# A hybrid decoder trunk: the convolution's inputs projected ahead of the index queries

## The chip, the cores and the metric

One core of a Trainium2 chip runs the whole program as one launch. The metric is the device time of that launch in microseconds, as the median of the runs shown. TensorE is called PE here, VectorE DVE, ScalarE ACT, GpSimd POOL and SyncE SP.

## The reference

Two layers work on 512 tokens of 1024 features, in float32. One projection of the normalized input gives every column that three token mixers need; their outputs are gated, summed and projected back, and a convolutional feed-forward block follows.

```python
z = h @ w_in + b_in
u_pool, u_conv, q, k, v, qi, ki, wi, gates = split_cols(z, IN_SIZES)
y_pool = pool_mixer(u_pool, pool_w, pool_scale) @ w_pool_out
y_conv = conformer_conv(u_conv, ...) @ ...       # GLU, 31 causal taps per channel, LayerNorm, silu
y_attn = dsa_attention(q, k, v, qi, ki, wi) @ w_attn_out
merged = g[:, :, 0] * y_pool + g[:, :, 1] * y_conv + g[:, :, 2] * y_attn
h = layer_norm(ALPHA * h + merged @ w_o);  h = layer_norm(ALPHA * h + conv_ffn(h))
```

In the attention an indexer scores all visible keys of a query with eight small heads, `sum_h w_h * relu(qi_h . ki)`; the best 128 keys are kept and only these take part in the softmax.

## The kernel before, in words

All activations lie with features on the partitions and the 512 tokens along the free axis. A product in float32 precision is made of three matmuls: each operand is split into a rounded high part and the rest, and hi x hi, hi x lo and lo x hi are added in PSUM (`proj`, L283 to L292). A weight chunk of 128 x 1024 gives one output tile of 128 columns: 8 steps of 3 matmuls, 24 in all. Weights come in the order of use from one tensor (`Weights`, L55): SP loads a chunk, ACT rounds it to `w_hi` (L74), DVE, or POOL for a few chunks, forms `w_lo` (L78). Four split chunks fit in SBUF, and a chunk is asked for two chunks ahead.

`mix` (L356) is the stage that the change touches. It projects, in this order: the index keys, the keys and the first half of the pooling channels (a head that starts while the norm before is still running); the four index query tiles, with 384 columns since the first 128 queries need no index; the second half of the pooling channels; two gate tiles and two value tiles of the convolution; the attention's values; then gate tiles and attention queries. A query or key tile is rotated (`rotate`, L411): ACT copies it, SP issues four transfers that swap half-heads, POOL multiplies by the sine (L408), DVE adds (L418), and ACT and DVE split the sum (`stack`, L423).

Beside these tiles run pieces of work that are written as generators and pumped by `step(ca, cb)`: `ca` is an amount for the index and attention work (`index_gen` L468, `attn_gen` L674), `cb` a number of pieces of the convolution (`conv_gen` L581). One piece of the convolution is one tap of one channel half. Of 31 taps the first is an ACT operation, every fourth is an accumulation on DVE in PSUM (L599, L602), and the others, 23 a half and 46 a layer, are a product on ACT (L596, two buffers `cvt`) and an addition on POOL (L597).

`pool_gen` (L510) makes the windowed sums of the pooling branch: per channel half a few additions on POOL (L517 to L527), a scaled subtraction on DVE (L529), a split (L534), three matmuls each into a bank `pb_p`, and a scaled split of the result into two `gbt` pairs, `pool_out` (L550, L551). `y_small` (L724) multiplies the output weights with `pool_out`; this happens first at L733, right behind the first gate tile (L732).

PSUM is handed out by tag: `pb_a` three banks, `pb_s` two (index and attention scores), `pb_p` two, `pb_v` one. `pb_p` serves every second query tile, the DVE taps' accumulator, `pool_gen`'s products, the transposed values and attention's transposes.

The framework takes the instructions in the order in which they are written as priorities, and sets the final order on each engine by a timeline of its own. On the chip each engine works through its list in that order.

Of the kernel before, what the change touches and what calls it, by code (L numbers as in the profile page):

```python
# [8 lines left out]
F32 = mybir.dt.float32  # L9
# [6 lines left out]
P = 128  # L16
# [73 lines left out]
def trunk_kernel(ctx, tc, x, positions, w, poolw, params, lnv, cons, out):  # L90
# [208 lines left out]
    def in_tile(c0=0, tag="a"):  # L299
        wt = W.take()  # L300
        o = bank(tag)
        in_part(o, wt, c0, c0, L)
        return o
# [52 lines left out]
    def mix(l, head, prev, ln, nxt):  # L356
        es = ExitStack()
        with es:
# [5 lines left out]
            def q_slot(tag, dt=F32R):  # L364
                return slot(tag, {"qa": 6, "qb": 4, "qc": 4}[tag], dt)

            def t_slot(dt=F32):
                return slot("t", 4, dt)
# [10 lines left out]
            def pb(ct):  # L379
                return par[:, l, PO_B + ct:PO_B + ct + 1]  # L380

            def hb(ct):
                return half_par[:, l, ct:ct + 1]
# [39 lines left out]
            def stack(a, s0, s1):  # L423
                for s, r, q in ((s0, UP, DN), (s1, DN, UP)):
                    A.activation(s[r], a[r], AF.Copy)
                    split_lo(s[q], a[r], s[r])
                return s0, s1
# [30 lines left out]
            up = [p_slot()]  # L458
            G.memset(up[0][:, 0:16], 0.0)
            A.activation(up[0][:, 16:], head.os[2], AF.Identity, bias=pb(6))  # L460
            for j in range(4):
                o = in_tile(P, "a" if j % 2 == 0 else "p")
                tag = "qa" if j < 2 else "qb"
                qi.append(stack(rotate(o, pb(2 + j), P, p_slot), q_slot(tag)[:, 0:L - P], q_slot(tag)[:, 0:L - P]))

            masks = [tri] + [None] * 3

# [89 lines left out]
                pass  # L557


            hp = []  # L560
            ths = []
            for c in range(2):
                o = in_tile()
                th = t_slot()
                A.activation(th, o, AF.Tanh, bias=hb(8 + c), scale=0.5)
                ths.append(th)
                step(3.0, 0)
            for c in range(2):
                o = in_tile()
                aa = t_slot()  # L570
                A.activation(aa, o, AF.Identity, bias=hb(10 + c), scale=0.5)
                hc = c_slot()[:, 0:CW - 1 + L]
                G.memset(hc[:, 0:CW - 1], 0.0)
                V.scalar_tensor_tensor(out=hc[:, CW - 1:], in0=ths[c], scalar=1.0, in1=aa,
                                       op0=ALU.add, op1=ALU.mult)
                hp.append(hc)
                step(2.5, 0)

            conv_out = []

            def conv_gen():  # L581
                accs = []
                for c in range(2):
                    acc, pacc = bank("p"), c_slot()[:, 0:L]

                    def tap(i):
                        k = PO_CW + c * CW + i
                        return par[:, l, k:k + 1]

                    A.activation(pacc, hp[c][:, 0:L], AF.Identity, scale=tap(0),  # L590
                                 bias=par[:, l, PO_CB + c:PO_CB + c + 1])
                    started = False
                    for i in range(1, CW):
                        if i % 4 != 0:
                            tm = slot("cvt", 2)
                            A.activation(tm, hp[c][:, i:i + L], AF.Copy, scale=tap(i))  # L596
                            G.tensor_tensor(out=pacc, in0=pacc, in1=tm, op=ALU.add)  # L597
                        elif not started:
                            V.tensor_scalar(acc, hp[c][:, i:i + L], tap(i), None, op0=ALU.mult)  # L599
                            started = True  # L600
                        else:
                            V.scalar_tensor_tensor(out=acc, in0=hp[c][:, i:i + L], scalar=tap(i),  # L602
                                                   in1=acc, op0=ALU.mult, op1=ALU.add)
                        yield 1
                    V.tensor_tensor(out=pacc, in0=acc, in1=pacc, op=ALU.add)
                    accs.append(pacc)
                    yield 1
                xn = []
                for bp in range(2):
                    pt = bank("p")  # L610
                    for bb in range(2):
                        b = bp * 2 + bb
                        for c in range(2):
                            T.transpose(pt[:, (bb * 2 + c) * P:(bb * 2 + c + 1) * P],
                                        accs[c][:, b * P:(b + 1) * P], ident)
                    xt = u_slot()
                    for bb in range(2):
                        seg = pt[:, bb * 256:(bb + 1) * 256]
                        st = sm.tile([P, 6], F32, name="c_st")
                        V.bn_stats(st, seg)  # L620
                        mv = sm.tile([P, 2], F32, name="ln_mv")
                        V.bn_aggr(mv, st)
                        ve = sm.tile([P, 1], F32, name="ln_ve")
                        V.tensor_scalar(ve, mv[:, 1:2], EPS, None, op0=ALU.add)
                        rs = sm.tile([P, 1], F32, name="ln_rs")
                        G.tensor_tensor(out=rs, in0=ve, in1=mhalf, op=ALU.pow)
                        V.tensor_scalar(xt[:, bb * 256:(bb + 1) * 256], seg, mv[:, 0:1], rs,
                                        op0=ALU.subtract, op1=ALU.mult)
                    xn.append(xt)
                    yield 1  # L630
                for c in range(2):
                    pt = bank("p")
                    for b in range(NB):
                        T.transpose(pt[:, b * P:(b + 1) * P],
                                    xn[b // 2][:, (b % 2) * 256 + c * P:(b % 2) * 256 + (c + 1) * P], ident)
                    hg = half_par[:, l, 41 + c:42 + c]
                    hbb = half_par[:, l, 43 + c:44 + c]
                    th = u_slot()
                    A.activation(th, pt, AF.Tanh, bias=hbb, scale=hg)
                    y2 = u_slot()  # L640
                    A.activation(y2, pt, AF.Identity, bias=hbb, scale=hg)
                    V.scalar_tensor_tensor(out=y2, in0=th, scalar=1.0, in1=y2, op0=ALU.add, op1=ALU.mult)
                    hi, lo = c_slot(F32R)[:, 0:L], c_slot(F32R)[:, 0:L]
                    A.activation(hi, y2, AF.Copy)
                    split_lo(lo, y2, hi)
                    conv_out.append((hi, lo))
                    yield 1

            bgb.append(conv_gen())


            o = in_tile()
            t = t_slot()
            A.activation(t, o, AF.Identity, bias=pb(12))
# [4 lines left out]
            vpv = vps.rearrange("p (b g d) -> p g b d", b=NB, g=2)  # L659
            A.activation(v_st[:, :, :, 0:64], vpv, AF.Copy)  # L660
            split_lo(v_st[:, :, :, 64:128], vpv, v_st[:, :, :, 0:64])
            step(1.5, 0)
            qa_hi = slot("qa_hi", 1, F32R, [P, 4, L])
            qa_lo = slot("qa_lo", 1, F32R, [P, 4, L])
            qa = (qa_hi, qa_lo)
# [170 lines left out]
def _chunks(a, np):  # L836
# [19 lines left out]
    for l in range(DEPTH):  # L856
# [6 lines left out]
            small.append(a[name][l].reshape(2, P, 2, 4, P).transpose(2, 1, 3, 0, 4).reshape(2, P, D))  # L863
        wa = a["w_attn_out"][l].reshape(2, 4, 64, D).transpose(1, 0, 2, 3).reshape(4, P, 4, 2, P)
        wa = wa.transpose(2, 1, 3, 0, 4).reshape(4, P, D)
        seq = [tiles[i] for i in (0, 1, 6, 2, 3, 4, 5) + tuple(range(7, 13))]
        for br in range(2):
            for hh in range(2):
                seq.append(small[br][hh])
# [66 lines left out]
```

## Time and profile before

| | us |
|---|---|
| median of 3 runs (1494.2 to 1494.74) | 1494.37 |
| the profiled execution, its own time | 1493.34 |
| its span | 1491.5 |
| PE busy | 1448.0 (97%) |
| DVE busy | 956.7 (64%) |
| ACT busy | 678.6 (45%) |
| POOL busy | 525.2 (35%) |
| DMA, mean over the span | 97 GB/s |

The span is the time from the first to the last instruction; the profiled execution's own time is 1.8 us longer. PE is counted busy as long as a matmul is in flight, and matmuls overlap, so its share says little: the number of matmuls started in a stretch says more. The mean granted clock of PE is 0.997 of full speed. The first layer's mixing stage lies at about 40 to 375 us, the second's at 770 to 1105 us.

### The profile page before, as it was taken

How to read it: one execution, taken by the hardware profiler on the slowest of the kernel's cores; microseconds unless marked ns; L12 is line 12 of the kernel's file. 1: busy time of each engine (PE TensorE's matmuls, PEld its weight loads, DVE VectorE, ACT ScalarE, POOL GpSimd, SP SyncE). 2: the span in 40 equal slices, each digit the busy share in tenths (PEclk: the TensorE clock that was granted, in tenths of full speed). 3: DMA queues.
4: the chain of work that ended last, by engine and by line, in shares of the span. 5: the costliest groups of instructions: out<-in, count | busy, mean ns of one | idle time of the engine just before them, and what ended most of it. 6: DMA issues, size and time to landing. Idle time of an engine off the chain costs nothing.

```text
span 1491.5 us, 18622 instructions
## 1 busy us (share of the span) xinstructions
PE 1448.0 (97%) x6850; PEld 1209.1 (81%) x6850; DVE 956.7 (64%) x1600; ACT 678.6 (45%) x1064; POOL 525.2 (35%) x395
## 2 busy tenths in 40 slices
PE   5999999999999999999999989999999999999997
PEld 5887878878888888888898878888788888888885
DVE  6789998746666555523267999966566655554234
ACT  5677555532544444421256774554334444443110
POOL 2459624129471111100133894220667311111004
PEclk9999999999999999999999999999999999999999
DMA  4432332223233323333224233222324333333331
GB/s 153 135 103 85 92 107 71 71 85 99 91 115 107 93 93 97 99 99 100 85 90 139 72 96 110 72 71 85 99 71 149 109 108 93 95 98 99 100 99 57
DMA packets 45019, 145.02 MB, mean 97 GB/s; under 512 B 6144, under 2 KB 7808, under 8 KB 44928
## 3 DMA queue, kind: packets, MB, share of 16 engines
q1 hardware_dynamic: 41472, 138.27, 30.3%
q10 hardware_dynamic: 3456, 5.57, 1.1%
q8 instruction: 54, 0.88, 0.2%
q14 instruction: 37, 0.30, 0.1%
HBM read 137.00 MB, written 2.10 MB: 93 GB/s over the span
## 4 chain that ended last, share of the span: by engine, by line
PE 81%; DVE 8%; ACT 4%; POOL 3%; issue 2%; DMA 1%; SPq 1%; POOLq 0%; DVEq 0%; ACTq 0%
PE pb_a L290 17%; PE pb_a L291 17%; PE pb_a L292 16%; PE pb_a L317 3%; PE pb_a L318 3%; PE pb_a L319 3%; POOL cv L597 2%; DVE w_lo L78 2%; PE pb_p L317 2%; PE pb_s L317 2%; PE pb_p L319 2%; PE pb_p L318 2%; PE pb_s L319 2%; PE pb_s L318 2%; DVE mask L492 1%
## 5 line engine op out<-in xcount | busy, mean ns | idle before, releaser
L78 DVE TENSOR_TENSOR w_lo<-w_raw,w_hi 128x1024 fp32r<-128x1024 f32 x210 | 289.4, 1379 | 362.4 <-ACT w_hi L74 362.1
L292 PE MATMUL pb_a<-hT_hi,w_lo 128*128 128x512 f32 (+1 forms) x1168 | 455.7, 390 | 4.3 <-DVE w_lo L78 4.3
L290 PE MATMUL pb_a<-hT_hi,w_hi 128*128 128x512 f32 (+1 forms) x1168 | 455.8, 390 | 1.3 <-DVE part L735 1.3
L291 PE MATMUL pb_a<-hT_lo,w_hi 128*128 128x512 f32 (+1 forms) x1168 | 455.4, 390 | 0.0
L74 ACT ACTIVATE w_hi<-w_raw 128x1024 fp32r<-128x1024 f32 x246 | 260.0, 1058 | 401.6 <-PE pb_a L291 159.6
L292 PEld LDWEIGHTS pb_a<-hT_hi,w_lo 128*128 128x128 f32 x1168 | 219.3, 188 | 48.9 <-DVE w_lo L78 6.0
L290 PEld LDWEIGHTS pb_a<-hT_hi,w_hi 128*128 128x128 f32 x1168 | 219.4, 188 | 45.4 <-DVE part L735 2.1
L291 PEld LDWEIGHTS pb_a<-hT_lo,w_hi 128*128 128x128 f32 x1168 | 219.4, 188 | 43.0
L78 POOL TENSOR_TENSOR w_lo<-w_raw,w_hi 128x512 fp32r<-128x512 f32 x72 | 96.6, 1364 | 265.8 <-ACT w_hi L74 265.8
L816 POOL TENSOR_TENSOR fu<-fu 128x512 f32<-128x512 f32 x44 | 63.8, 1451 | 350.4 <-DVE fu L807 350.4
L597 POOL TENSOR_TENSOR cv<-cv,cvt 128x512 f32<-128x512 f32 x92 | 134.1, 1459 | 36.8 <-ACT cvt L596 31.4
L596 ACT ACTIVATE cvt<-cv,par 128x512 f32<-128x512 f32 x92 | 65.5, 719 | 30.3 <-POOL cv L597 30.1
L815 ACT ACTIVATE fu<-fu 128x512 f32<-128x512 f32 x44 | 27.8, 631 | 80.8 <-DVE fu L807 80.7
L807 DVE SCALAR_TENSOR_TENSOR fu<-pb_a,par,fu 128x510 f32<-128x510 f32 x82 | 61.4, 749 | 2.7
L804 ACT ACTIVATE fu<-pb_a,par 128x512 f32<-128x512 f32 x82 | 62.4, 761 | 0.6 <-DVE g_lo L112 0.6
L805 DVE SCALAR_TENSOR_TENSOR fu<-pb_a,par,fu 128x511 f32<-128x511 f32 x82 | 60.9, 743 | 0.0
L217 POOL TENSOR_TENSOR h<-h,gbt 128x512 f32<-128x512 f32 x32 | 55.3, 1752 | 14.0 <-DMA gbt<-in_lnv_dram 14.0
L771 POOL TENSOR_TENSOR part<-part,t 128x512 f32<-128x512 f32 x16 | 27.3, 1705 | 78.0 <-DVE t L770 78.0
L205 ACT ACTIVATE gbt<-pb_a,par 128x128 f32<-128x128 f32 x96 | 35.8, 469 | 39.9 <-PE pb_a L197 39.9
L491 DVE MAX8 m<-mask 128x8 f32<-128x256 f32 (+2 forms) x96 | 53.0, 554 | 1.2
L492 DVE MATCH_REPLACE8 mask<-m,mask 128x256 f32<-128x256 f32 (+2 forms) x96 | 52.0, 542 | 0.0
L317 PE MATMUL pb_a<-w_hi,g_hi 128*128 128x512 f32 x132 | 51.3, 389 | 0.0
(305 smaller groups left out, 2652.1 us busy)
## 6 DMA issues: line engine op xcount, KB each, us to landing
w_raw<-in_w_dram SPq DMA_DIRECT2D x246, 512.0 KB, 3.6
gbt<-in_lnv_dram ACTq DMA_DIRECT2D x20, 256.0 KB, 3.3
h<-in_x_dram SPq DMA_DIRECT2D x4, 512.0 KB, 5.4
t<-t SPq DMA_DIRECT2D x32, 64.0 KB, 2.0
out_dram<-h SPq DMA_DIRECT2D x8, 256.0 KB, 2.0
part<-t SPq DMA_DIRECT2D x32, 48.0 KB, 2.5
part<-t SPq DMA_DIRECT2D x16, 64.0 KB, 2.0
par<-in_params_dram SPq DMA_DIRECT2D x2, 143.5 KB, 6.2
```

The costliest lines, as they stand in the source:

```text
L74: nc.scalar.activation(hi, raw, AF.Copy)
L78: eng.tensor_tensor(out=lo[:, cs], in0=raw[:, cs], in1=hi[:, cs].bitcast(F32), op=ALU.subtract)
L290: T.matmul(o, wh, xh(xc), start=(i == 0), stop=False)
L291: T.matmul(o, wh, xl(xc), start=False, stop=False)
L292: T.matmul(o, wl, xh(xc), start=False, stop=(i == n - 1))
L317: first = T.matmul(po[b], lh(k, b), wh, start=(k == 0), stop=False)
L318: T.matmul(po[b], lh(k, b), wl, start=False, stop=False)
L319: T.matmul(po[b], ll(k, b), wh, start=False, stop=(k == nk - 1))
L492: V.match_replace(out=sc, in_to_replace=m8, in_values=sc, imm_value=FILL)
L596: A.activation(tm, hp[c][:, i:i + L], AF.Copy, scale=tap(i))
L597: G.tensor_tensor(out=pacc, in0=pacc, in1=tm, op=ALU.add)
L816: G.tensor_tensor(out=ys[1], in0=ys[0], in1=ys[1], op=ALU.mult)
```

## The change

Three things are moved. The four tiles of the convolution's inputs, with the code that starts `conv_gen`, now come before the four index query tiles. The taps are pumped from there on: three behind each query tile, four behind the second pooling tile, four behind the values, then as before in the loop over the gates. And the weights are laid out in that order. Index work is no longer pumped behind the convolution's tiles, and gets 4.0 instead of 1.5 behind the values. No operation is added or left out.

```diff
             A.activation(up[0][:, 16:], head.os[2], AF.Identity, bias=pb(6))
-            for j in range(4):
-                o = in_tile(P, "a" if j % 2 == 0 else "p")
...
-            bga.extend(index_gen(i) for i in range(1, NB))
...
-            for _ in pool_gen():
-                pass
-
             hp = []
             ths = []
             for c in range(2):
                 o = in_tile()
                 th = t_slot()
                 A.activation(th, o, AF.Tanh, bias=hb(8 + c), scale=0.5)
                 ths.append(th)
-                step(3.0, 0)
             for c in range(2):
                 o = in_tile()
...
                 hp.append(hc)
-                step(2.5, 0)
...
             bgb.append(conv_gen())
 
+            for j in range(4):
+                o = in_tile(P, "a" if j % 2 == 0 else "p")
+                tag = "qa" if j < 2 else "qb"
+                qi.append(stack(rotate(o, pb(2 + j), P, p_slot), q_slot(tag)[:, 0:L - P], q_slot(tag)[:, 0:L - P]))
+                step(0, 3)
...
+            bga.extend(index_gen(i) for i in range(1, NB))
...
+            for c in range(1, 2):
+                o = in_tile()
...
+                step(2.0, 4)
...
+            for _ in pool_gen():
+                pass
...
             o = in_tile()
             t = t_slot()
...
-            step(1.5, 0)
+            step(4.0, 4)
...
-        seq = [tiles[i] for i in (0, 1, 6, 2, 3, 4, 5) + tuple(range(7, 13))]
+        seq = [tiles[i] for i in (0, 1, 6, 8, 9, 10, 11, 2, 3, 4, 5, 7, 12)]
```

Line numbers of the moved code differ between the two kernels: a tap on POOL is L597 before and L497 after, its product on ACT L596 and L496, `pool_gen`'s additions L517 to L527 and L608 to L618, its result L550 and L641, the index scores L476, L477 and L567, L568, the copy of the transposed values L660 and L659.

On POOL, in the first layer's mixing stage, the rows of before from the first index query's rotation (L408 with 384 columns) to the taps:

```order
L408 TENSOR_TENSOR part<-part,sinT 128x384 x3
L504 MEMSET part 128x16
L517 TENSOR_TENSOR part<-part 128x527
L520 COPY part<-part 64x512
L521 TENSOR_TENSOR part<-part 64x525
L408 TENSOR_TENSOR part<-part,sinT 128x384
L517 TENSOR_TENSOR part<-part 128x527
L524 TENSOR_TENSOR part<-part 128x525
L525 TENSOR_TENSOR part<-part 128x521
L526 COPY part<-part 64x512
L527 TENSOR_TENSOR part<-part 64x512
L597 TENSOR_TENSOR cv<-cv,cvt 128x512 x25
```

All rotations and all of `pool_gen` stand ahead of the first tap. Now, at the same place, the list begins with taps:

```order
L497 TENSOR_TENSOR cv<-cv,cvt 128x512 x7
L408 TENSOR_TENSOR part<-part,sinT 128x384
L497 TENSOR_TENSOR cv<-cv,cvt 128x512 x2
L408 TENSOR_TENSOR part<-part,sinT 128x384
L497 TENSOR_TENSOR cv<-cv,cvt 128x512 x2
L408 TENSOR_TENSOR part<-part,sinT 128x384
L497 TENSOR_TENSOR cv<-cv,cvt 128x512 x8
```

Behind these 19 taps come the three operations of `pool_gen`'s first half (L608, L611, L612), and then, on the same engine:

```order
L497 TENSOR_TENSOR cv<-cv,cvt 128x512
L408 TENSOR_TENSOR part<-part,sinT 128x384
L497 TENSOR_TENSOR cv<-cv,cvt 128x512
L608 TENSOR_TENSOR part<-part 128x527
L497 TENSOR_TENSOR cv<-cv,cvt 128x512
L615 TENSOR_TENSOR part<-part 128x525
L497 TENSOR_TENSOR cv<-cv,cvt 128x512 x2
L616 TENSOR_TENSOR part<-part 128x521
L497 TENSOR_TENSOR cv<-cv,cvt 128x512
L617 COPY part<-part 64x512
L618 TENSOR_TENSOR part<-part 64x512
L497 TENSOR_TENSOR cv<-cv,cvt 128x512 x20
```

The last operation of `pool_gen` (L618, L527 before) now has 25 taps ahead of it, where it had none. The second layer's list is the same.

On PE, around the first matmul with `pool_out` (`gbt`), in the kernel before; `hT` is the normalized input, and such a triple belongs to a tile of the input projection:

```order
L476 MATMUL pb_s<-qa 128x384
L477 MATMUL pb_s<-qa 128x384
L290 MATMUL pb_a<-hT_hi,w_hi 128x512
L291 MATMUL pb_a<-hT_lo,w_hi 128x512
L292 MATMUL pb_a<-hT_hi,w_lo 128x512
L290 MATMUL pb_a<-gbt,w_hi 128x512
L290 MATMUL pb_a<-hT_hi,w_hi 128x512
```

and in the changed one, where `part` is the input of `pool_gen`'s products:

```order
L567 MATMUL pb_s<-qa 128x384
L568 MATMUL pb_s<-qa 128x384
L292 MATMUL pb_p<-part 128x512 x2
L567 MATMUL pb_s<-qa 128x384
L568 MATMUL pb_s<-qa 128x384
L567 MATMUL pb_s<-qa,qb 128x384
L568 MATMUL pb_s<-qa,qb 128x384
L290 MATMUL pb_a<-gbt,w_hi 128x512
L290 MATMUL pb_a<-hT_hi,w_hi 128x512
```

In both, the next gate tile begins right behind that first matmul; in the changed kernel the rows ahead of it are short ones, the tiles of the input projection that stood among them are done earlier.

On ACT, from the copies of `pool_out` (L641) to the copy of the transposed values (L659), in the changed kernel:

```order
L641 ACTIVATE gbt<-pb_p,par 128x512
L496 ACTIVATE cvt<-cv,par 128x512
L570 ACTIVATE u<-pb_s 128x384
L641 ACTIVATE gbt<-pb_p,par 128x512
L570 ACTIVATE u<-pb_s 128x384
L496 ACTIVATE cvt<-cv,par 128x512 x4
L659 ACTIVATE vst<-pb_p 128x8x64
```

Before, 12 of a layer's products of taps stood ahead of that copy in the first layer; now 37 do, in both layers.

## Rows read from the trace of the kernel before

**Rows 1.** Windows: us, then busy (xcount) of PE, PEld, DVE, ACT, POOL, PEclk, DMA.
```profile
40.00:97.00 57.00, 56.31 (x287) 49.36 (x286) 43.85 (x62) 37.89 (x61) 25.54 (x20) 1.00 0.45 137
97.00:150.00 53.00, 51.33 (x227) 41.62 (x227) 51.81 (x108) 40.14 (x63) 49.60 (x35) 1.00 0.26 80
150.00:217.00 67.00, 64.96 (x301) 53.01 (x300) 64.35 (x153) 34.27 (x57) 34.10 (x28) 1.00 0.34 98
450.00:500.00 50.00, 50.00 (x222) 41.42 (x221) 29.82 (x35) 22.39 (x30) 7.28 (x5) 1.00 0.34 99
```

**Rows 2.** Waits of PE over the span: releaser, us in total, times, longest.
```profile
PE pb_a L290 <- ACT qa_hi L710: 5.3, 2, 2.6
PE pb_a L292 <- DVE w_lo L78: 4.3, 4, 1.8
...
PE pb_a L290 <- ACT cv L644: 1.3, 1, 1.3
PE pb_a L290 <- DVE part L735: 1.3, 2, 0.7
```

**Rows 3.** Timeline of PE, both layers: start us, us, engine, line, operation.
```profile
45.30 0.33 PE L290 MATMUL pb_a<-hT_hi,w_hi 128*128 128x384 f32 x1
45.48 0.34 PE L291 MATMUL pb_a<-hT_lo,w_hi 128*128 128x384 f32 x1
45.74 0.35 PE L444 MATMUL pb_p<-ident,t 8*128 8x8 f32 x3
...
103.04 0.40 PE L290 MATMUL pb_a<-gbt,w_hi 128*128 128x512 f32 x1
...
775.96 0.35 PE L444 MATMUL pb_p<-ident,t 8*128 8x8 f32 x3
...
834.71 0.39 PE L290 MATMUL pb_a<-gbt,w_hi 128*128 128x512 f32 x1
```

**Rows 4.** Timelines of ACT and POOL: the first convolution input, and taps.
```profile
84.84 0.67 ACT L571 ACTIVATE t<-pb_a,half_par 128x512 f32<-128x512 f32 x1
...
88.76 3.01 POOL L597 TENSOR_TENSOR cv<-cv,cvt 128x512 f32<-128x512 f32 x2 [13.11 <-ACT cvt L596]
...
99.48 7.71 POOL L597 TENSOR_TENSOR cv<-cv,cvt 128x512 f32<-128x512 f32 x5 [0.44 <-ACT cvt L596]
...
131.61 9.53 POOL L597 TENSOR_TENSOR cv<-cv,cvt 128x512 f32<-128x512 f32 x7
```

**Rows 5.** Timeline of POOL: first and last operation of each half of pool_gen.
```profile
63.78 1.06 POOL L517 TENSOR_TENSOR part<-part 128x527 f32<-128x527 f32 x1
...
65.58 1.06 POOL L521 TENSOR_TENSOR part<-part 64x525 f32<-64x525 f32 x1
...
68.56 1.06 POOL L517 TENSOR_TENSOR part<-part 128x527 f32<-128x527 f32 x1
...
74.37 1.28 POOL L527 TENSOR_TENSOR part<-part 64x512 f32<-64x512 f32 x1
```

**Rows 6.** Groups of POOL by line and form, whole span: busy us, mean ns.
```profile
L597 POOL TENSOR_TENSOR cv<-cv,cvt 128x512 f32<-128x512 f32 x92 | 134.1, 1459 | 36.8 <-ACT cvt L596 31.4
...
L408 POOL TENSOR_TENSOR part<-part,sinT 128x384 f32<-128x384 f32 x8 | 11.8, 1476 | 21.8 <-DMA part<-t 17.6 <-DVE qa L112 4.0
```

**Rows 7.** Timelines of DVE and ACT: pool_gen's second half.
```profile
86.71 0.75 DVE L529 SCALAR_TENSOR_TENSOR u<-part,cst 128x512 f32<-128x512 f32 x1
...
89.69 0.91 DVE L112 TENSOR_TENSOR part<-u,part 128x512 fp32r<-128x512 f32 x1
...
99.85 0.68 ACT L550 ACTIVATE gbt<-pb_p,par 128x512 fp32r<-128x512 f32 x1
```

**Rows 8.** Window behind PE's wait for the merged attention, first layer (columns of rows 1).
```profile
317.00:321.00 4.00, 3.26 (x9) 2.59 (x10) 0.72 (x2) 0.63 (x1) 0.00 (x0) 0.57 0.37 131
```

**Rows 9.** Timeline of DVE: a weight split with POOL idle, and one among taps.
```profile
84.96 1.23 DVE L78 TENSOR_TENSOR w_lo<-w_raw,w_hi 128x1024 fp32r<-128x1024 f32 x1 [1.67 <-ACT w_hi L74]
...
123.56 2.08 DVE L78 TENSOR_TENSOR w_lo<-w_raw,w_hi 128x1024 fp32r<-128x1024 f32 x1 [0.53 <-ACT w_hi L74]
```

More of the change, by code (lines that the diff above doesn't have):

```diff
@@ L460, in mix @@
             A.activation(up[0][:, 16:], head.os[2], AF.Identity, bias=pb(6))
+            hp = []
+            ths = []
+            for c in range(2):
+                o = in_tile()
+                th = t_slot()
+                A.activation(th, o, AF.Tanh, bias=hb(8 + c), scale=0.5)
+                ths.append(th)
+            for c in range(2):
+                o = in_tile()
+                aa = t_slot()
+                A.activation(aa, o, AF.Identity, bias=hb(10 + c), scale=0.5)
+                hc = c_slot()[:, 0:CW - 1 + L]
+                G.memset(hc[:, 0:CW - 1], 0.0)
+                V.scalar_tensor_tensor(out=hc[:, CW - 1:], in0=ths[c], scalar=1.0, in1=aa,
+                                       op0=ALU.add, op1=ALU.mult)
+                hp.append(hc)
@@ L461, in mix @@
+            bgb.append(conv_gen())
             for j in range(4):
@@ L557, in mix @@
                 pass
[L560 to L566, printed above, removed]
-                step(3.0, 0)
[L568 to L576, printed above, removed]
-                step(2.5, 0)
@@ L579, in mix @@
[L579 to L647, printed above, removed]
@@ L649, in mix @@
-            bgb.append(conv_gen())
             o = in_tile()
```

66 lines of the change are left out of this document (added).

## The prediction

> **What bounds the kernel now.** I read the table of windows first, because PE is called busy nearly everywhere. In a feed-forward stretch, 450 to 500 us, 222 matmuls of 512 columns start in 50.00 us, which is 0.225 us each: that is the pace of a PE that waits for nothing [rows 1]. The mixing stages come close to it. In them DVE is the next limit (51.81 of 53.00 us from 97 to 150, 64.35 of 67.00 from 150 to 217), with POOL at 49.60 of 53.00 in the first of these. Early in the stage, 40 to 97 us, POOL has only 25.54 of 57.00 us of work. Then the waits of PE: between its head and its tail there is little to win. The wait for the merged attention (ACT qa_hi) is 2 times 2.6 us, the waits for w_lo, for the pooled partial sums (DVE part) and for the convolution output (ACT cv) are 4.3, 1.3 and 1.3 us in both layers together [rows 2]. Everything else in the mixing stages is PE work that the change does not alter. So a change of order can give back some 10 us at most, while a new wait of PE costs its full length. The question is therefore which stream PE will wait for.
>
> **The step to follow.** Call y0 the first matmul of the pooling branch's output projection (L290 with a "gbt" operand, the two gbt pairs being pool_out). It starts at 103.04 us in the first layer and at 834.71 in the second [rows 3]. In the order of both programs the next gate tile stands right behind y0's first matmul on PE, and nothing of it ahead. PE takes its queue in order, so once the tiles ahead of y0 are done, y0's start moves everything.
>
> y0 needs pool_out, and that hangs on POOL: eight small additions and copies of pool_gen, the last of them L527. In the kernel before, POOL does them at 63.78 to 75.65 us, idles, and begins the convolution's taps only at 88.76 us [rows 4, 5]. After the change the order on POOL is different: 25 of the layer's 46 taps and all four rotations stand ahead of the last pool_gen operation. This is what the change adds to the path.
>
> **Cost of y0, first layer.** (a) The work ahead on PE is the same up to the three small transposes L444, at 45.74 us, except that 23 matmuls there now have 512 columns where they had 384: 0.225 against 45.48 - 45.30 = 0.18 us [rows 3], 0.05 us each, 1.2 us in all, so 46.9. (b) The tile of the first convolution input is complete 1 + 24 + 24 = 49 matmuls later, 49 x 0.225 = 11.0, so 57.9. (c) From the copy of that tile on ACT (84.84) to the first tap on POOL (88.76) took 3.9 us [rows 4], so POOL starts at 61.8. (d) Its queue from there: 25 taps at their mean of 1.459 = 36.5, four rotations at 1.476 = 5.9 [rows 6]; pool_gen's first half from 63.78 to 66.64 (2.9) and its second from 68.56 to 75.65 (7.1) [rows 5]. Together 52.4, so 114.2. (e) From the scaled subtraction on DVE (86.71) to the end of the split (89.69 + 0.91) is 3.9; three matmuls 0.7 and the copy of pool_out on ACT 0.68 follow [rows 7]: 5.3, so y0 at 119.5. That is 16.5 us later than 103.04. Two pairs of index matmuls of 384 columns more stand ahead of y0 than before, 4 x 0.18 = 0.7 us, which need not be done later: **15.8 us**.
>
> Second layer: 775.96 for L444 [rows 3], 11 wider matmuls 0.6, then 12 + 24 + 24 = 60 matmuls 13.5, then the same 3.9 + 52.4 + 5.3: 851.7, which is 17.0 after 834.71, less 0.7: **16.3 us**.
>
> Bounds of this term. A tap is 9.53 / 7 = 1.36 us where seven ran in a row; the first eleven took from 88.76 to 99.48 + 7.71 = 107.19, 1.68 each, with their waits for ACT [rows 4]. That moves y0 by -2.5 or +5.5 us. Beside it POOL may start 2 us sooner and (e) be 2 us shorter, where DVE's queue is emptier. So 9 to 22 us a layer.
>
> **The first query tile.** Its PSUM tag pb_p has two banks; the DVE taps' accumulator holds one, and the transposed values hold the other until ACT copies them (vst). In the new order this copy stands behind the 37th of the taps' products on ACT, which reuses the buffer that POOL's 35th tap frees. Ten taps after 114.2 is 128.8; a product, the copy and the split (0.68, 0.68 and 0.75, by rows 7's copy and DVE operation) make it 130.9. PE has 30 matmuls to do from y0 to there, 6.8 us, 126.3. It waits **4.6 us**, in each layer; 0 if POOL keeps ahead, 7 at 1.68 a tap.
>
> **The clock.** After the wait of 2.63 us ahead of the merge, the granted clock over the next 4.00 us was 0.57 [rows 8], so part of it ran at 1.2 instead of 2.4 GHz: 4.00 x 0.43 = 1.7 us. A wait of 15 us should do the same once a layer: **1.7**; 0 to 3.4.
>
> **The end of attention.** The new order leaves six of attention's value blocks without gate tiles between them at the end of the stage, where two stood so before. A block alone is a copy, a split and two matmuls, 0.68 + 0.75 + 0.45 = 1.9 us; two run at a time, and PE's own share is at least 0.45. Four blocks more cost between 0 (hidden) and 4 x 1.45 = 5.8 us; I take **1.0**, nearer to the hidden end, because two blocks overlap.
>
> **What is won.** Taps leave the crowded stretch, so DVE is ahead of PE when w_lo is wanted. Of the 6.9 us of waits for w_lo, part and cv I take half, **3.4 us** in both layers; 0 to 6.9. The rest is free: the weights' new order is the order of use, with the same number of DMAs, and each rotation's four transfers on SP stand behind weight loads as before; POOL's last taps come earlier, off the path.
>
> **Sum.** 15.8 + 16.3 + 2 x (4.6 + 1.7 + 1.0) - 3.4 = 43.3 us. The profiled execution took 1493.34 us (span 1491.5), 1.03 us less than the median of the runs, 1494.37. The median moves to about **1538 us**.
>
> **The rivals.**
> *Short queue.* The taps run at 1.36 us, POOL starts sooner, the query waits for nothing, all waits go: 2 x 9 - 6.9 = +11, **1505 us**. For it: in the early stretch POOL has room [rows 1]. Against it: DVE and ACT work on weights and rotations there, and the first eleven taps of before were the slow ones.
> *Blocked taps.* The taps now run beside the weight splits. DVE's w_lo took 1.23 us at 84.96, while POOL was idle, and 2.08 us at 123.56, among taps [rows 9]; if in the early stretch every tap is as slow as those first eleven, y0 comes 5.5 us later and the query 2.2 us, per layer: +15.4, **1553 us**. The Trainium skill, "SBUF — State Buffer", section "Who interferes with whom", has a rule for this: a GpSimd operation and a VectorE operation with two SBUF inputs exclude each other for the whole instruction. By it the eight weight splits that fall among the 25 taps would each hold POOL up for a split's length, about 8 x 1.23 = 10 us a layer in the worst case, against 5.5 by the rows; the trace agrees in direction, in the 1.23 against 2.08 us.
> *DVE relieved, faster.* If DVE's full stretch from 97 to 217 us is what really holds PE, taking twenty taps out of it removes the 6.9 us, and one of the two waits for the merged attention becomes cover for the other's work: 6.9 + 2.6 + 1.7 of clock = 11 us, **1483 us**. It decides if pool_out is ready when PE arrives, at 103.04: POOL would have to be done 5.3 us earlier, at 97.7, which leaves 97.7 - 61.8 - 15.9 = 20.0 us for 25 taps, 0.80 each. No tap row is near that.
> *No change.* The waits won (6.9) and a small delay of y0 cancel, or the taps do not really move: y0 would be about 3.5 us late in each layer, 0.96 us a tap. The order on POOL speaks against both.
>
> **How the numbers follow.** A difference of 0.2%, 3 us, is what can be told from none. Forecast (slower by 25 to 55 us) 0.53, blocked taps or worse 0.18, short queue 0.18, relieved 0.07, no change 0.04. So slower 0.89, same 0.04, faster 0.07. The range leaves out the last two and the far ends of the others: from 1507, just above the short queue's figure, to 1562.
>
> **What would show it.** In the profile after: y0's first matmul near 119 and 852 us, with a wait of PE for ACT (pool_out) of over 10 us in each layer, longer than any wait now; POOL busy without a gap from about 62 us, with the taps ahead of the last pool_gen operation; a second, shorter wait of PE at the first query tile; a low granted clock after the long wait; shorter waits for w_lo. It is wrong if y0 starts within 5 us of before, if POOL shows gaps between 62 and 114 us, or if PE waits there for weights instead.

## The result, and the profile after

The changed kernel takes **1540.63 us** (median of 4 runs, 1539.47 to 1541.2), the kernel before 1494.28 beside it (4 runs, 1492.47 to 1494.74): a ratio of **1.0307**, 95% interval 1.0293 to 1.0321, so 46.35 us slower. The profiled execution took 1539.47 us, its span is 1537.7 us, the mean granted clock 0.980.

From the page of the changed kernel, the table of engines and two lines of the 40 slices (38.4 us each):

```profile
PE 1458.7 (95%) x6850; PEld 1215.8 (79%) x6850; DVE 960.5 (62%) x1600; ACT 683.5 (44%) x1064; POOL 521.3 (34%) x395
...
PE   5967999999999999999999599999999999999997
...
PEclk9987999999999999999999699999999999999999
```

PE has two holes, in the third and fourth slice and in the 23rd, one in each layer, and its clock falls there. They lie where both mixing stages compute their index scores. The windows that answer to [rows 1], and two short ones inside the first hole:

```profile
40.00:97.00 57.00, 55.06 (x281) 48.36 (x280) 36.88 (x44) 39.84 (x58) 32.28 (x23) 1.00 0.41 122
97.00:150.00 53.00, 33.17 (x132) 26.37 (x131) 43.02 (x80) 34.20 (x58) 48.89 (x38) 0.74 0.19 55
150.00:217.00 67.00, 67.00 (x305) 55.34 (x304) 57.54 (x118) 29.80 (x42) 19.28 (x17) 1.00 0.35 105
...
103.00:111.00 8.00, 0.00 (x0) 0.00 (x0) 6.98 (x9) 4.08 (x8) 7.92 (x6) 0.57 0.42 140
...
118.00:130.00 12.00, 6.73 (x17) 5.01 (x18) 10.27 (x18) 7.12 (x15) 9.79 (x8) 0.50 0.05 13
```

From 97 to 150 us PE starts 132 matmuls where it started 227. For 8 us it starts none, while POOL is busy for 7.92 of them. Behind it, from 150 to 217 us, PE has no idle time at all. The waits of PE over the span, to be read against [rows 2]:

```profile
PE pb_s L567 <- DVE qb L112: 18.4, 4, 9.4
PE pb_s L567 <- ACT u L570: 18.2, 4, 5.5
...
PE pb_s L567 <- DVE qa L112: 4.1, 4, 1.7
PE pb_a L290 <- ACT qa_hi L709: 4.1, 2, 2.1
...
PE pb_v L702 <- DVE o L706: 2.2, 2, 1.1
PE pb_p L290 <- DVE mask L579: 2.1, 2, 1.0
```

The new waits, 40.7 us in both layers, stand at L567, an index score: for the split of an index query (qb, qa) and for the relu that empties the scores' bank (u). No wait names pool_out; the last line shown, 1.0 us in each layer, stands at the first of `pool_gen`'s products. The waits for w_lo, cv and part (L735) are gone, and those for the merged attention went from 5.3 to 4.1 us. PE's timeline, with y0 as its last row:

```profile
111.20 0.58 PE L567 MATMUL pb_s<-qa,qb 128*128 128x256 f32 x1 [9.36 <-DVE qb L112]
...
118.60 0.69 PE L567 MATMUL pb_s<-qa 128*128 128x384 f32 x1 [5.49 <-ACT u L570]
...
123.24 0.69 PE L567 MATMUL pb_s<-qa 128*128 128x384 f32 x1 [3.63 <-ACT u L570]
...
125.28 0.80 PE L290 MATMUL pb_p<-part 128*128 128x512 f32 x1 [1.04 <-DVE mask L579]
...
129.93 0.63 PE L290 MATMUL pb_a<-gbt,w_hi 128*128 128x512 f32 x1
```

y0 is 26.89 us later than in [rows 3]; in the second layer it starts at 882.53, 47.82 later. Three landmarks of PE split the loss (us, layer 1 / layer 2):

| start of | before | after |
|---|---|---|
| y0 | 103.04 / 834.71 | 129.93 / 882.53 |
| first 512-column query tile | 113.66 / 844.49 | 137.92 / 890.18 |
| first matmul on the merged attention ("merge") | 317.74 / 1048.75 | 341.38 / 1093.39 |
| last matmul of the program | 1480.93 | 1527.08 |

Up to y0 the first layer loses 26.89; from y0 to the merge it wins 3.25 (211.45 for 214.70); from there to the second layer's y0 24.18 are lost; then 3.18 won, and 1.51 lost up to the end: 46.15 us. **All of the loss lies ahead of y0**, some 25 us a layer.

Why index scores wait is on the three other engines. POOL first:

```profile
65.09 2.66 POOL L497 TENSOR_TENSOR cv<-cv,cvt 128x512 f32<-128x512 f32 x2 [14.07 <-ACT cvt L496]
...
105.25 1.45 POOL L408 TENSOR_TENSOR part<-part,sinT 128x384 f32<-128x384 f32 x1
...
116.12 1.26 POOL L497 TENSOR_TENSOR cv<-cv,cvt 128x512 f32<-128x512 f32 x1
...
118.00 1.26 POOL L618 TENSOR_TENSOR part<-part 64x512 f32<-64x512 f32 x1
```

The fourth index query's rotation (105.25) stands behind 20 taps, pool_gen's last addition (118.00) behind 25; in [rows 5] the latter started at 74.37. PE's first wait, of 9.36 us, ends 4.5 us after that rotation, with the split of its query. Of the rotation's lateness POOL's queue itself holds only some 3 us (an estimate: its last transfer was issued at 100.5, and these land 1.9 us later). PE had projected this query only at 90.39, and ACT copied it at 98.11, behind products that wait for POOL. Then ACT and DVE:

```profile
115.19 0.72 ACT L496 ACTIVATE cvt<-cv,par 128x512 f32<-128x512 f32 x1 [0.50 <-POOL cv L497]
117.42 0.72 ACT L496 ACTIVATE cvt<-cv,par 128x512 f32<-128x512 f32 x1 [1.51 <-POOL cv L497]
...
118.17 0.38 ACT L570 ACTIVATE u<-pb_s 128x256 f32<-128x256 f32 x1
...
122.80 0.39 ACT L570 ACTIVATE u<-pb_s 128x256 f32<-128x256 f32 x1 [1.44 <-DVE pb_v L575]
```

```profile
119.30 1.85 DVE L620 SCALAR_TENSOR_TENSOR u<-part,cst 128x512 f32<-128x512 f32 x1 [4.65 <-POOL part L618]
121.19 1.12 DVE L622 TENSOR_TENSOR u<-part,cst 128x16 f32<-128x16 f32 x1
122.23 0.48 DVE L575 SCALAR_TENSOR_TENSOR pb_v<-u,wq,pb_v 128x256 f32<-128x256 f32 x1
122.62 1.02 DVE L623 TENSOR_TENSOR u<-u,part 128x16 f32<-128x16 f32 x1
```

The relu at 118.17 is that of the scores which PE had finished at 112.0 (111.58 + 0.42 on its timeline). It stands on ACT behind tap products, and the last three of these wait until POOL frees one of the two cvt buffers; the product at 117.42 ends at 118.14, and the relu follows. The next relu needs a free u buffer, so a score accumulation on DVE (L575, 122.23), and that stands behind pool_gen's scaled subtraction (L620), which waited 4.65 us for POOL. Neither relu nor accumulation uses anything of the convolution or the pooling: **they wait because of what is ahead of them in their queue**. The Trainium skill, "PSUM — Partial Sum Buffer", section "Engine vs sequencer instructions", calls the queues of ScalarE, VectorE and GpSimd strict FIFO; these rows agree.

From pool_gen's end on POOL (118.00 + 1.26 = 119.26) the rows follow one another to y0: L620 to L623 on DVE, the splits on ACT and DVE, pool_gen's products on PE from 125.28 on, the copy of pool_out on ACT (129.03 to 129.71), y0 at 129.93. PE's wait of 1.04 us at 125.28 is put down to L579, but that product doesn't use its result; the split of the pooling weights on ACT (L633), which it does use, ended at 125.23 too. So **the last wait ahead of y0 is for the pooling, and the index scores' waits end 1 us before it**.

### The profile page after: what moved, and what is told of

It is laid out like the page before. It is cut to its first block, busy times and chain, and to the rows that moved or that the text cites. A ratio compares the mean times of both kernels' runs of the same rounds, so it can differ in the third digit from the quotient of the medians.

```text
span 1537.7 us, 18632 instructions
## 1 busy us (share of the span) xinstructions
PE 1458.7 (95%) x6850; PEld 1215.8 (79%) x6850; DVE 960.5 (62%) x1600; ACT 683.5 (44%) x1064; POOL 521.3 (34%) x395
## 3 DMA queue, kind: packets, MB, share of 16 engines
q10 hardware_dynamic: 3456, 5.57, 1.1%
## 4 chain that ended last, share of the span: by engine, by line
PE 87%; POOL 4%; DVE 3%; issue 2%; ACT 2%; DMA 1%; POOLq 0%; ACTq 0%; DVEq 0%
PE pb_a L290 18%; PE pb_a L291 18%; PE pb_a L292 18%; PE pb_a L317 3%; PE pb_a L319 3%; PE pb_a L318 3%; POOL cv L497 2%; PE pb_p L317 2%; PE pb_s L317 2%; PE pb_p L319 2%; PE pb_s L319 2%; PE pb_p L318 2%; PE pb_s L318 2%; PE pb_p L290 1%; PE pb_p L291 1%
## 5 line engine op out<-in xcount | busy, mean ns | idle before, releaser
L292 PEld LDWEIGHTS pb_a<-hT_hi,w_lo 128*128 128x128 f32 x1168 | 219.5, 188 | 43.3
L497 POOL TENSOR_TENSOR cv<-cv,cvt 128x512 f32<-128x512 f32 x92 | 131.3, 1428 | 41.3 <-ACT cvt L496 36.9
L496 ACT ACTIVATE cvt<-cv,par 128x512 f32<-128x512 f32 x92 | 65.1, 720 | 31.6 <-POOL cv L497 31.1
L688 ACT ACTIVATE qa<-qa,mx 128x128 f32<-128x128 f32 (+3 forms) x64 | 35.7, 559 | 43.8 <-DVE mx L685 41.3
```

The costliest lines, as they stand in the source:

```text
L292: T.matmul(o, wl, xh(xc), start=False, stop=(i == n - 1))
```

## The experiments

The theories at the start: (Q) POOL's queue, with taps ahead of rotations and pool_gen, is the whole loss, as predicted; (A) ACT's tap products hold the index operations up; (T) the tiles' new order costs by itself; (P) the pumps placed by hand do it. y0 and the merge below are those of the first layer.

**1. Without the early pumps.**

```diff
-                step(0, 3)
+                step(0, 0)
...
-                step(2.0, 4)
+                step(2.0, 0)
```

> The changed kernel, with the conv inputs first as it has them, but with no pieces of the convolution pumped before pool_gen (three per index query tile and four behind the second pooling tile are written as zero; the first pump is the one behind the values). In the order on POOL 25 taps still stand ahead of pool_gen's last sum, since the framework fills POOL with whatever is ready. Theory (POOL's queue is what counts, and the early inputs alone fill it): 1536 to 1546 us, first matmul on pool_out at 127 to 133 us, as in the changed kernel. Rival (the pumps placed by hand bring the loss): 1490 to 1505 us, that matmul at 103 to 110 us.

Measured: 1535.5 us, ratio 1.0271 (1.0256 to 1.0287), y0 at 128.83. The time is 0.5 us below the theory's range, y0 inside it. P falls: the tap spreading that the change writes is worth some 5 us, as the two ratios stand to each other. The order on POOL is still filled with 25 taps by the framework, because their input is there; it is the place of the four input tiles that counts. The fourth rotation comes at 95.26 here, 10 us earlier than in the changed kernel, and y0 only 1.1 us: the rotation doesn't set y0. pool_gen's end on POOL, 118.16, does: y0 follows it by 10.67 us, as in the changed kernel.

**2. The kernel before with the last pump alone.**

```diff
-            step(1.5, 0)
+            step(4.0, 4)
```

> The kernel before, with only the pump behind the values changed from (1.5, 0) to (4.0, 4). Theory: no tap comes ahead of pool_gen on POOL, first matmul on pool_out at 103 +- 1 us; 1490 to 1497 us, no difference from before beyond 0.2%. Rival (more index and convolution work behind the values costs or gains by itself): over 4 us to either side.

Measured: 1497.39 us, ratio 1.0018 (1.0008 to 1.0027), y0 at 102.40. That is 2.6 us slower, 0.4 us above the theory's range and at the border of what can be told from no change; y0 is not late, so the pump is no part of the hole ahead of it.

**3. All taps wait for pool_gen.** Tiles and weights as in the changed kernel.

```diff
-                G.memset(hc[:, 0:CW - 1], 0.0)
...
+                    G.tensor_tensor(out=hp[c][:, 0:CW - 1], in0=gate[1][:, 16:16 + CW - 1],
+                                    in1=gate[1][:, 16:16 + CW - 1], op=ALU.subtract)
```

> The changed kernel with its order of tiles and weights, but every tap of the convolution made to wait for pool_gen: the 30 columns of zeros ahead of the convolution's input are written by POOL from pool_gen's last sum minus itself, and no pieces are pumped earlier. No tap stands ahead of a rotation or of pool_gen on POOL. Theory (the taps in the queues ahead of these are the whole loss): first matmul on pool_out at 102 to 108 us in the first layer, 1490 to 1503 us. Rival (the tiles' and weights' new order delays the index queries or the second pooling tile by itself): that matmul still later than 115 us, 1515 us or more.

Measured: 1519.52 us, ratio 1.0165 (1.015 to 1.018), y0 at 111.93. Between the two theories. 18.0 of y0's 26.89 us go with the taps; 8.9 stay, though pool_gen is done at 95.68 and all rotations by 88.5. So a third stays with the new order of the tiles (T). PE's waits from 97 to 112 us:

```profile
PE pb_s L568 <- ACT u L571: 5.3, 3, 2.1
PE pb_p L290 <- ACT part L636: 0.4, 1, 0.4
```

With the convolution's tiles done, the last index scores come with no tile between them, and each pair waits for the relu of the pair two ahead. The waits shown are 5.7 of the 8.9 us; behind them the granted clock is 0.50 from 102 to 112 us. The rest of this kernel's loss is later: its taps end at 182.06 in place of 167.54, and from y0 to the merge it takes 221.24 us, 6.54 more than before.

**4. Half of POOL's additions.**

```diff
-                            G.tensor_tensor(out=pacc, in0=pacc, in1=tm, op=ALU.add)
+                            if c == 1:
+                                G.tensor_tensor(out=pacc, in0=pacc, in1=tm, op=ALU.add)
```

> The changed kernel without the 23 additions on POOL of the first channel half (left out of the computation); the products on ACT and the taps on DVE all stay. In the order on POOL 10 taps stand ahead of pool_gen's last sum in place of 25, and one ahead of the fourth rotation in place of 20. Theory (POOL's queue): it is 15 x 1.46 = 22 us shorter, first matmul on pool_out at 106 to 113 us, 1496 to 1512 us. Rival (the tap products on ACT hold up its queue, whoever adds them): the matmul at 120 us or later, 1520 us or more.

Measured: 1531.5 us, ratio 1.0247 (1.023 to 1.0264), y0 at 124.36. With POOL's list 15 taps shorter, 22 us were expected back; 5.6 came. The longest wait named is a relu again:

```profile
PE pb_s L568 <- ACT u L571: 32.3, 6, 9.6
```

But y0 still follows pool_gen's end on POOL (113.69) by 10.67 us. That end came only 5.57 us earlier, because POOL's second half of pool_gen stands behind seven taps, and these, with their waits for products on ACT, take POOL until 104.61, though its input was ready at 91.47.

**5. None of POOL's additions.** The same line taken out for both halves.

> The changed kernel without any of the 46 additions on POOL (left out of the computation); the products on ACT and the taps on DVE all stay, and no product ever waits for POOL. Theory (POOL's queue, and ACT's products that wait for POOL): first matmul on pool_out at 106 to 115 us in the first layer, as where the taps waited for pool_gen (111.9), and 1495 to 1512 us. Rival (it is ACT's own time for some 25 products of 0.72 us ahead of the index scores that delays PE, whoever adds them): 118 us or later, 1520 us or more.

Measured: 1518.45 us, ratio 1.0155 (1.014 to 1.017), y0 at 119.13. The time is 1.6 us below the rival's range, y0 in it. POOL has no tap left, pool_gen ends at 99.53, and y0 is still 16.1 us late, as A has it. ACT's timeline shows where:

```profile
104.91 6.84 ACT L496 ACTIVATE cvt<-cv,par 128x512 f32<-128x512 f32 x11
...
112.26 0.37 ACT L569 ACTIVATE u<-pb_s 128x256 f32<-128x256 f32 x1
```

Eleven products in a row and a twelfth at 111.65, which wait for nobody, and then the relu. PE's longest wait in this stage is for it, 7.78 us.

**6. None of ACT's products.**

```diff
-                            tm = slot("cvt", 2)
-                            A.activation(tm, hp[c][:, i:i + L], AF.Copy, scale=tap(i))
-                            G.tensor_tensor(out=pacc, in0=pacc, in1=tm, op=ALU.add)
+                            G.tensor_tensor(out=pacc, in0=pacc, in1=hp[c][:, i:i + L], op=ALU.add)
```

> The changed kernel with the 46 products on ACT left out (the scale of these taps is left out of the computation): POOL adds the shifted input itself, so ACT never waits for POOL's buffers. In the order on POOL 34 taps stand ahead of pool_gen's last sum and 25 ahead of the fourth rotation, more than in the changed kernel (25 and 20). Theory A (POOL's queue alone is enough): fourth rotation after 105 us, pool_gen done at 122 us or later, first matmul on pool_out at 128 us or later. Theory B (the wait comes about because ACT's index operations stand behind products that wait for POOL): without products that matmul at 110 to 120 us.

Measured: 1547.82 us, ratio 1.0353 (1.0338 to 1.0369), y0 at 133.09, fourth rotation at 106.41, pool_gen done at 123.18. ACT's products are gone and nothing is won: theory A of this run holds, POOL's queue alone is enough. It is no clean measure of ACT's queue, since 34 taps, for 25, now stand ahead of pool_gen's end, which comes 3.9 us later. y0 follows that end by 9.91 us. How it reaches the index scores without ACT's products, on ACT and on DVE:

```profile
126.49 0.39 ACT L568 ACTIVATE u<-pb_s 128x256 f32<-128x256 f32 x1 [14.29 <-DVE pb_v L573]
```

```profile
123.22 1.68 DVE L618 SCALAR_TENSOR_TENSOR u<-part,cst 128x512 f32<-128x512 f32 x1 [10.90 <-POOL part L616]
124.93 0.95 DVE L620 TENSOR_TENSOR u<-part,cst 128x16 f32<-128x16 f32 x1
125.91 0.49 DVE L573 SCALAR_TENSOR_TENSOR pb_v<-u,wq,pb_v 128x256 f32<-128x256 f32 x1
```

DVE stands 10.90 us at the scaled subtraction of the pooling; the score accumulation is behind it, the relu waits for that, and PE waits 13.12 us for the relu.

**7. The pooling tile first.** The second pooling tile and pool_gen move ahead of the convolution's inputs.

```diff
-        seq = [tiles[i] for i in (0, 1, 6, 8, 9, 10, 11, 2, 3, 4, 5, 7, 12)]
+        seq = [tiles[i] for i in (0, 1, 6, 7, 8, 9, 10, 11, 2, 3, 4, 5, 12)]
```

> The changed kernel with the second pooling tile, and pool_gen with it, moved ahead of the convolution's inputs (the weights in that order). pool_gen then stands ahead of all taps on POOL; 24 taps still stand ahead of the fourth rotation. Theory (PE waits for the fourth index query and for the index scores first; pool_out is only the next in line): pool_gen done at 75 to 85 us, fourth rotation after 100 us, first matmul on pool_out at 115 to 127 us, 1515 to 1538 us. Rival (pool_out is what PE is held by, as predicted): that matmul at 104 to 110 us, 1493 to 1506 us.

Measured: 1518.02 us, ratio 1.0156 (1.0139 to 1.0173), pool_gen done at 58.87, fourth rotation at 114.07, y0 at 106.88, first query tile at 123.14, merge at 327.56. The expectation's landmark failed: y0 came in the rival's range because PE's order now has it ahead of several index scores, so it says little. The time and the merge, still 9.8 us late, say that pool_out complete at 81.77, 25 us ahead of y0, doesn't cure the kernel: half of the loss stays (23 us for 46). How much of what is left belongs to the rotation, to ACT or to the tiles' order is not separated here.

**8. The pooling tile first, the taps after the fourth rotation.** Number 7 with the wait of number 3, on the rotation's result.

> As the run with the pooling tile first, and every tap made to wait for the fourth index query's rotation (the zeros ahead of the convolution's input are written by POOL from that rotation's result minus itself). Nothing on POOL stands behind a tap before the first matmul on pool_out. Theory (with both queues clear only the tiles' order is left): that matmul at 104 to 112 us, 1500 to 1518 us. Rival (the tiles' order alone costs as much as where the taps waited for pool_gen, 25 us, whatever the pooling does): 1519 us or more.

Measured: 1507.03 us, ratio 1.0079 (1.0064 to 1.0094), y0 at 100.61, first query tile at 107.47, merge at 324.62. y0 is 3.4 us earlier than the theory had it, the time in its range. PE loses nothing early, and 13 us between the query tile and the merge (217.15 for 204.08): the taps end at 180.77, and PE waits 4.79 us at 164 for a relu that stands at 168.66 on ACT, behind six products, each of which waits for POOL.

**9. Neither products nor POOL's additions.** Numbers 5 and 6 together; the taps on DVE stay.

> The changed kernel without the 46 products on ACT and without the 46 additions on POOL (both left out of the computation; the taps on DVE stay). Theory (two queues in order, POOL's and ACT's, each enough to hold PE: without POOL's additions the first 512-column query tile came at 125.97 us, without ACT's products at 144.13): with both gone it comes at 113 to 121 us, about where the taps waited for pool_gen (121.41), and the time is 1495 to 1512 us. Rival (something else of the new order, such as the index scores in one bunch, holds PE as long as without POOL's additions): the query tile at 124 us or later, 1515 us or more.

Measured: 1505.22 us, ratio 1.0078 (1.0061 to 1.0095), y0 at 111.05, query tile at 118.25. With both queues clear 18.9 of the 26.89 us are back, where clearing POOL alone gave 10.8 and clearing ACT alone, with POOL's queue longer, nothing. 8.0 stay, as 8.9 did in number 3, with the new order of the tiles; 5.4 of them are waits for relus, which stand behind a weight's rounding on ACT and pool_gen's own operations on ACT and DVE, and the clock is 0.66 from 102 to 112 us.

**10 and 11. Eight, or eleven, early taps.** Number 8, with the wait put into one column and ahead of tap 11 (or 15) of the first half only.

```diff
+                        if c == 0 and i == 11:
+                            G.tensor_tensor(out=hp[0][:, CW - 2:CW - 1], in0=gate[:, 0:1],
+                                            in1=gate[:, 0:1], op=ALU.subtract)
```

> As the run with the pooling tile first and the taps last, but the first 10 taps of the first channel half (8 on POOL) need not wait; the others wait for the fourth rotation through one column of the convolution's input. POOL was idle there from about 60 to 81 us, and eight taps take 8 x 1.46 = 12 us. Theory (early taps are free as far as POOL is idle and no index operation stands behind them; what was lost late came from taps that ended 13 us later than in the kernel before): first query tile at 106 to 110 us, last tap done at 166 to 172 us, 1490 to 1501 us. Rival (any early tap delays the rotations or the index scores by as much as it wins later): 1504 us or more.

> As the run before it with 14 early taps (11 on POOL): four of them stand between the first and the second rotation, so the second to fourth rotation come some 4 us later than with eight. Theory: query tile at 108 to 114 us, last tap 4 us earlier, 1490 to 1503 us, within 4 us of the run with eight. Rival (the rotations are what counts, one for one): 1505 us or more.

Measured: 1528.47 us, ratio 1.0231 (1.0216 to 1.0246), and 1546.02 us, ratio 1.0342 (1.0322 to 1.0362). The times are in the rivals' ranges, but not by their mechanism. The fourth rotation came at 112.55 and 112.95, some 18 us later than in number 8 (94.36), and nearly the same in both kernels, so it doesn't follow the number of early taps. POOL's and PE's timelines of number 10:

```profile
112.55 1.02 POOL L408 TENSOR_TENSOR part<-part,sinT 128x384 f32<-128x384 f32 x1 [14.19 <-DMA part<-t]
```

```profile
99.60 0.69 PE L290 MATMUL pb_p<-hT_hi,w_hi 128*128 128x384 f32 x1 [0.96 <-DVE qa L112]
```

POOL is idle for 14.19 us ahead of it, because PE projects the fourth index query only at 99.60. A DVE tap at 80.88 (L560) opens its accumulator in one of the two pb_p banks, and it stays open until the half is done; the second and fourth index query share the other bank, one full rotation apart. That is read from the rows; a third bank wasn't tried, and why eleven cost 17 us more than eight stays open.

**12. The kernel before with the pooling tile first.** The one candidate for beating it.

```diff
-        seq = [tiles[i] for i in (0, 1, 6, 2, 3, 4, 5) + tuple(range(7, 13))]
+        seq = [tiles[i] for i in (0, 1, 6, 7, 2, 3, 4, 5) + tuple(range(8, 13))]
```

> The kernel before, with the second pooling tile and pool_gen moved ahead of the four index query tiles (the weights in that order); the index queries stay ahead of the convolution's inputs, and no tap stands ahead of a rotation or of pool_gen on POOL. Theory (where the pooling tile came first and the taps waited for the rotations, the first 512-column query tile came at 107.47 us, 6 us before that of the kernel before, and the loss came later from taps that ended at 181 us): query tile at 106 to 113 us, last tap done at 164 to 171 us, merge at 311 to 318 us, 1483 to 1495 us, the one version with a chance to beat the kernel before. Rival (pooling first delays the index queries by a tile, 5.4 us, and gives that on): 1498 us or more.

Measured: 1519.4 us, ratio 1.0163 (1.015 to 1.0177), query tile at 124.02, last tap at 182.53, merge at 331.19. The expectation failed: PE now does pool_gen's product at once, and waits for its operands:

```profile
71.11 0.80 PE L290 MATMUL pb_p<-part 128*128 128x512 f32 x1 [4.60 <-ACT part L501]
```

There is no wait for relus among PE's waits, but also no gain. Waits for weights came back too (w_lo 6.5 us, w_hi 4.7 us in both layers, for 4.3 and none before). How the 25 us split among these isn't separated. None of the twelve beats the kernel before.

## Why the prediction was right, and which step of it was not

**The total and its sign were right**: 43.3 us forecast, 46.35 measured, inside 1507 to 1562. The first statement, that only some 10 us can be won and that a new wait of PE costs its full length, held. The place held too: taps ahead of the rotations and pool_gen on POOL, a hole ahead of y0 in both layers. But the sum came out near by luck, because two errors cancel.

**Cost of y0, the step that failed.** Forecast 15.8 and 16.3 us with bounds of 9 to 22, measured 26.89 and 24.18: outside the bounds, and 19.0 us too little in both layers. The path was the right one: POOL's queue, then pool_gen's steps on DVE, ACT and PE. Its terms, first layer: POOL started at 65.09, not 61.8. The queue (d) was nearly right, 54.2 us for 52.4, with pool_gen done at 119.26. Step (e) was given 5.3 us and took 10.67: L620 1.85 for 0.75, L622 1.12 and L623 1.02 for 0.17 each, ACT's splits and copy behind tap products, index scores between pool_gen's products, and PE at half clock. These three misses make up 10.4 us. In the second layer (e) took 10.50, and is most of the miss there too. (In PE's timeline of the first layer one 384-column pair of index scores more stands ahead of y0 than before, not two.)

Where taps stand ahead of pool_gen's end on POOL, y0 follows that end by nearly the same time (the first four rows; us, first layer). Where none do, number 9 has a like time, and in numbers 5 and 3 other waits hold y0:

| | pool_gen done on POOL | y0 | difference |
|---|---|---|---|
| changed kernel | 119.26 | 129.93 | 10.67 |
| 1, no early pumps | 118.16 | 128.83 | 10.67 |
| 4, half of POOL's additions | 113.69 | 124.36 | 10.67 |
| 6, no products | 123.18 | 133.09 | 9.91 |
| 9, neither products nor POOL's additions | 100.02 | 111.05 | 11.03 |
| 5, no additions on POOL | 99.53 | 119.13 | 19.60 |
| 3, taps behind pool_gen | 95.68 | 111.93 | 16.25 |

What the prediction left out is a second path beside this one. It has PE get through all that stands ahead of y0 and then wait for pool_out alone, over 10 us in each layer. That sign didn't come: PE waits for index scores instead, which stand behind tap products on ACT and behind the pooling's subtraction on DVE, and these wait for POOL. pool_out is ready just as PE gets there. In the changed kernel the second path ends 1 us ahead of the first. It counts as soon as the first is shortened: by the predicted chain alone number 5 would have brought y0 to some 105 (99.53 and 5.3), and it came at 119.13. By numbers 3 and 9, 18 to 19 us of the first layer's 26.9 go when the taps are out of the queues, and 8 to 9 stay with the order of the tiles, for which the prediction had 1.2 us, for wider matmuls.

**The first query tile**, forecast to wait 4.6 us in each layer: no wait. From y0 it takes 7.99 and 7.65 us, less than the 10.62 and 9.78 of before. With PE late by 27 us, the taps had probably run far enough; no run tests that.

**The clock**, 1.7 us a layer: right in kind. The granted clock is 0.57 from 103 to 111 us, in which PE does nothing, and 0.50, its lower level of 1.2 GHz, from 118 to 130. Until 125.28 PE mostly waits anyway. From there to 131.21 it starts 15 matmuls in 5.93 us, those of 512 columns some 0.43 us apart, for 0.225; at the prediction's 0.225 and 0.18 us they would take 3.1. So the clock costs some 2.8 us here, an estimate from these rows, and 2.2 of it lie ahead of y0, in the 26.89. Behind the merge, where [rows 8] had 0.57, it is now 1.00:

```profile
341.00:345.00 4.00, 3.62 (x15) 2.85 (x16) 0.70 (x2) 0.33 (x1) 0.00 (x0) 1.00 0.00 0
```

**What is won, and the end of attention.** Half of 6.9 us was counted as won; all of it was: the waits for w_lo, cv and part are gone. The end of attention, 1.0 us a layer, has 1.1 (DVE o L706) against 0.6 won on qa_hi. From y0 to the merge 6.43 us were won in both layers, where the terms between them (4.6, 1.0, and the 3.4) gave 7.8 lost. This error of 14.2 us hid most of the other.

**The rivals.** *Blocked taps* (1553) lies 12 us above, and its mechanism didn't come: the 25 taps ahead of pool_gen's end took 36.9 us, 1.48 each, for the 36.5 of the forecast. *Short queue* missed, as did *DVE relieved*: DVE is relieved and PE is without a wait from 150 to 217 us, which goes with the 6.4 us above. *No change* didn't come.

## What to carry to other kernels

Where a stream of work is moved, write down for each engine that it uses what will stand behind it in the queue, and ask for each such row who waits for it, also for rows that have nothing to do with the stream. A path followed along one chain of data gives the price of one queue; here POOL's, ACT's and DVE's all held the same engine: clearing POOL's of taps alone gave back 40% of the delay of y0, clearing ACT's and POOL's 70%. Ask also which wait ends last: PE's named waits are for index scores, but y0 followed POOL's last addition by the same 10.67 us in three kernels. And see whether a piece of code that is moved changes the order at all: with a scheduler that fills idle engines, the place of the inputs decided it, and the pumps hardly.

## What the runs showed of the hardware

A tiny operation on DVE with two SBUF inputs can cost nearly as much as the POOL operations beside it. pool_gen's 16-column operations took 0.17 us in the kernel before, and 1.12 and 1.02 us among taps; the subtraction over 512 columns 0.75 and 1.85. Number 5, whose POOL has no taps in the same order of tiles, has the old durations again:

```profile
105.67 0.74 DVE L619 SCALAR_TENSOR_TENSOR u<-part,cst 128x512 f32<-128x512 f32 x1
106.45 0.17 DVE L621 TENSOR_TENSOR u<-part,cst 128x16 f32<-128x16 f32 x1
```

The accumulation of a score, with one SBUF tensor and its other operand in PSUM, takes 0.48 us with taps beside it (122.23 above) as without. The Trainium skill, "SBUF — State Buffer", section "Who interferes with whom", has a GpSimd operation that reads SBUF and a VectorE operation with two SBUF inputs shut each other out for the whole instruction. The rows agree, and both sides pay: beside a weight split on DVE that took 2.09 us (98.11, for 1.22 at other times), pool_gen's first addition on POOL took 2.00 us (99.12), for 1.06 in [rows 5].
